# Two-layer encoder trunk: x's norms one group earlier, the second layer's rotary tables under the output projection, six weight tiles in flight between the layers

## The chip, the cores and the metric

The kernel runs on one core of a Trainium2 chip. The metric is the time of one execution on the device in microseconds (us). Its engines are named as the profile names them: PE (TensorE, matmuls), PEld (its weight loads), DVE (VectorE), ACT (ScalarE), POOL (GpSimd) and SP (SyncE, which here only issues transfers). Each engine takes its own instructions strictly in the order in which the program lists them, and waits where one needs a result that is not there yet.

## What is computed

Input x is 512 tokens of 1024 float32 values; there are 256 memory tokens. Each of two layers normalises x, multiplies it by one input projection, attends, gates the heads' outputs and adds an output projection to x:

```python
for i in range(DEPTH):                      # DEPTH = 2
    h = rmsnorm(x, norm_g[i])
    mem_h = rmsnorm(mem, mem_norm_g[i])
    if i % 2 == 0:
        proj = h @ w_in_a                   # 3 x 3 x 8 heads of 128, q_mem, gate
        o_mix = mixer_dilated(qkv, qn_a, kn_a, ang_a)
    else:
        proj = h @ w_in_b                   # 8 query heads, 2 kv heads, q_mem, gate
        o_mix = mixer_axial_gqa(q, k, v, qn_b, kn_b, ang_b)
    o_mem = memory_attention(q_mem, mem_h, w_mem_kv[i], ...)   # 4 heads
    y = concatenate([o_mix, o_mem]) * silu(gate)
    x = x + y @ w_out[i]
```

The rotary tables of the second layer are products of cosines and sines with the gains `qn_b` and `kn_b`.

## The kernel before

**Products.** A float32 product is made of three passes on PE: an operand is split into a rounded part and a rest, and `mm3` (L164 to L166) multiplies high by high, high by low and low by high. A weight tile (128x1024) is loaded by an SP transfer (`wl`, L238), rounded by ACT (`wh`, L287) and its rest is made by DVE (`wo`, L297). L164 and L166 need `wh`; L165 needs `wo`. Four pairs of `wh` and `wo` exist at a time.

**Seven products instead of eight.** Each projection of 512 columns is a Strassen-like scheme (`s_chunk`): seven products on quarters, in the order 12, 11, S1, S2, S4, S3, 22. Sums of weight quarters are made by accumulating transfers of POOL. Sums of the activation's quarters are made once per layer: `first_t` (quarters 12 and 11, tokens blocks 0 and 1), `diffs_t` (L531 makes S1, L532 makes S3, token blocks 2 and 3) and `rest_t` (L544 makes S2, L545 makes S4; then ACT rounds each at L539 and DVE makes its rest at L540). S1, S2, S3 and S4 are called `fS`, `f` and after rounding `hS` in the profile's rows. ACT copies a finished bank (`sn`, L364) and DVE adds into such a copy (`sn`, L381). The bank of product 11 is used again by S2, which therefore waits for L381.

**The order of the work.** Nothing reorders instructions after the program is written. A small driver does it while the program is built: after each group of PE matmuls it advances a slot counter, and generators that are due write their next piece into the engines' queues. `yield n` means "go on n slots later". What stands in one slot and what in the next thus sets each engine's order.

**The start.** Four groups of 12 matmuls make the memory keys, four the memory values (`mem_kv`, `proj_t`, operand `act`), while `prep` normalises the four token blocks of x: `norm_1` squares and sums on ACT (`sq`, L462) and gets the inverse root on POOL, `norm_2` scales on DVE (`x`, L469). PE then transposes a block (`xT`, L475, eight transposes into two PSUM buffers), ACT rounds it (L158) or copies it (L522, L527), and DVE makes the rest (L161). Between these PE also transposes the memory keys (`qT`, L571, one PSUM buffer each, read by ACT L619 and DVE L620). `xT` and `qT` share four PSUM buffers named `at`. `ahead` runs hooks inside the first four groups.

**Between the layers.** The output projection (`out_proj`) is a seven-product chunk with `y` and then two chunks on the third quarter of `y` (`out_rest`, results added at L739). Then come the second layer's memory keys and values, and the first chunk of its input projection. The second layer's tables (`setup_b`, one product at L1262 and four at L1265) are made on DVE in slots after the output projection.

**Weights in flight.** `KEEP` gives, by kind of chunk, how many weight tiles may be loaded and not yet used: `O1` is `out_rest`, `T2b` the second layer's memory keys and values.

Of the kernel before, what the change touches and what calls it, by code (L numbers as in the profile page):

```python
# [21 lines left out]
TCKW = {}  # L22
NBIG, NM4, NS2, SCRATCH = 7, 23, 13, 2048
RING, LEAD = 4, 2
BULK, ACTIVE, SET_AT, WARM, MEM_B, PREP_Y, ACC_AT, PREP_B, HALF, SET_B = 2, 2, 15, 1, 12, 1, 4, 1, {"a": 3, "b": 3, "o": 0}, 1
MEM_STEP = 1, 1
MEM_D = 4
PD = 2
# [7 lines left out]

SEQ = [1, 2, 0] + list(range(3, len(PLAN)))
T1_DMA = 17
KEEP = {"T2": 8, "T2b": 4, "O1": 4, "W1": 9, "W2": 10, "W2s": 9, "W1b": 7, "W2b": 9}


class Driver:
# [83 lines left out]
def trunk_kernel(ctx: ExitStack, tc: tile.TileContext, x, mem, wall, norm_g, mem_norm_g, gcol,  # L126
# [14 lines left out]
    def m4(dt=F32, name="m4"):  # L141
        return pool.tile([128, 1024], dt, tag="m4", name=name, bufs=NM4)
# [213 lines left out]
    def s_chunk(n, act, ev, tokens=True, pre=None, half=False, soon=False):  # L356


        units, per = n // 256, 1024 // n
        bank, snap = [None, None], {}  # L360

        def keep(name, u, b):
            t = snap[name, u] = s2(name="sn")
            A.copy(t, b)  # L364
            yield 1
            if name == "s3":
                diff(u)
                yield 1
                yield from ev("22", u, snap["s5", u])

        def diff(u):

            if (u, "22") not in snap:
                c = snap[u, "22"] = snap["s5", u]
                V.tensor_tensor(c, c, snap["s3", u], ALU.subtract)  # L375

        def add(q, name, u, b):
            t = snap[name, u]
            if name == "s3":
                diff(u)  # L380
            V.tensor_tensor(t, b, t, ALU.subtract if q == "12" else ALU.add)  # L381
            yield 1
            yield from ev(q, u, t)

        after = ((keep, "z"), (add, "11", "z"), (keep, "s5"), (keep, "s2"), (add, "12", "s2"), (keep, "s3"), (add, "21", "s3"))
        for i, (a, s, fresh) in enumerate(PRODUCTS):
            while a not in act:
                drv.tick()
            if fresh:
                bank[s] = [pj() for _ in range(units)]  # L390
            for x in range(units):
                wh, wo = [t.rearrange("p (k c) -> p k c", c=n) for t in W.take()]
                ah, al = act[a][:, 0], act[a][:, 1]
                for b in range(2):
                    if pre and i == x == 0 and b:
                        pre()
                    if half and b:
                        n_half[0] += 1
                        if n_half[0] % half == 0:
                            drv.half()  # L400
                    o = bank[s][b] if units == 2 else bank[s][0][:, b * 256:(b + 1) * 256]
                    bs = slice(b * 128, (b + 1) * 128)
                    for k in range(per):
                        kk = x * per + k
                        st, sp = fresh and kk == 0 and (units == 2 or b == 0), kk == 3
# [61 lines left out]
    def norm_2(xb, r, row, js=(0, 1)):  # L467
        for j in js:
            V.scalar_tensor_tensor(xb[j], xb[j], r, row[j], ALU.mult, ALU.mult)  # L469
# [65 lines left out]
    def rest_t(H, c, ds):  # L535

        def put(k, f):
            hi, lo = slot(H, k, c)
            A.copy(hi, f)  # L539
            drv.late(lambda: V.tensor_tensor(lo, f, hi.bitcast(F32), ALU.subtract))  # L540
# [12 lines left out]
        yield 1  # L553
# [24 lines left out]
    def halves(t):  # L578
        return [t[:, 0:512], t[:, 512:1024]]
# [261 lines left out]

        return gate, prep_y, YW, ys

    def out_proj(YW, ys, src, evac, tiles, half=False):

        acc, done = {}, set()

        def load():
            for i in range(2):
                for u, t in enumerate(tiles()):  # L850
                    nc.sync.dma_start(t, src[2 * i + u])
                    acc[2 * i + u] = halves(t)
                yield 2

        def ev(q, u, t):
            b, n = 2 * (int(q[0]) - 1) + u, int(q[1]) - 1
# [15 lines left out]
    rows = {}  # L872
# [17 lines left out]
        if c % 2:  # L890
            W.dma(2)
    H, H2 = {}, {}
    xb = [halves(t) for t in xt]
# [58 lines left out]
    def ahead(u, b):  # L952

        if (u, b) == (0, 1):
            for j in range(2):
                A.copy(rows["x"][j], gain[j])
            norm_3(mb[1], M, 128, 0)
            for c in range(2):
                norm_2(mb[c], nst[c], first, (1,))
        if (u, b) == (1, 0):  # L960
            for c in range(2):
                norm_3(mb[c], M, 128 * c, 1)
# [283 lines left out]
                yield EO[2]  # L1246
                yield from rest_t(H2, b - 2, EO[3:])

    drv.spawn(mem_norm(1), MEM_B)
    out_proj(YW, ys, xv, ev_o, lambda: [m4(name="acc") for _ in range(2)])  # L1250

    ropeB = pool.tile([128, 2048], F32, tag="tabs", name="tabs", bufs=1).rearrange("p (a c b e) -> p a c b e", a=2, c=2, b=4)
    tb_raw = s2(name="tbraw").rearrange("p (c b e) -> p c b e", c=2, b=4)
    nc.sync.dma_start(tb_raw, tab_b.rearrange("p (c b e) -> p c b e", c=2, b=4))
    grB = s2(name="grB")[:, 0:256].rearrange("p (a e) -> p a e", a=2)
    nc.sync.dma_start(grB[:, 0], qn_b.to_broadcast([128, 128]))
    nc.sync.dma_start(grB[:, 1], kn_b.to_broadcast([128, 128]))

    def setup_b():
        V.tensor_scalar(grB[:, 0], grB[:, 0], QS, None, ALU.mult)  # L1262
        for qk in range(2):
            for cs_ in range(2):
                V.tensor_tensor(ropeB[:, qk, cs_].rearrange("p b (h e) -> p b h e", h=2),  # L1265
                                tb_raw[:, cs_, :, None, :].to_broadcast([128, 4, 2, 64]),
                                grB[:, qk].rearrange("p (h e) -> p h e", h=2)[:, None].to_broadcast([128, 4, 2, 64]), ALU.mult)
# [45 lines left out]
    def rope_b(t, qk, i, d):  # L1313

        def v(x):
            return x.rearrange("p (b h e) -> p b h e", b=2, h=2)

        ta, sb = s2(name="ta"), s2(name="sb")
        V.tensor_tensor(v(ta), v(t), ropeB[:, qk, 0, 2 * i:2 * i + 2, None, :].to_broadcast([128, 2, 2, 128]), ALU.mult)
        V.tensor_tensor(v(sb), v(t), ropeB[:, qk, 1, 2 * i:2 * i + 2, None, :].to_broadcast([128, 2, 2, 128]), ALU.mult)  # L1320
# [235 lines left out]
```

## Time and profile before

| | us |
|---|---|
| three timed runs | 968.25, 972.17, 972.54 |
| their median | 972.17 |
| the profiled execution | 966.39 |
| span of its instructions | 964.6 |

The span runs from the first to the last instruction of the profiled execution; 1.8 us of it lie outside. A row of the timeline gives the start, the duration, the engine, the line, the operation, what is written and read, and in brackets the idle time just before it and what ended it. Rows merged as "x2" are two instructions back to back. A view by windows gives each engine's busy time in a stretch with the number of instructions, the granted clock of PE as a share of full speed, the share of the transfer engines in use and GB/s.

### The profile page before, as it was taken

Reading aid. Unit: us, or ns where it says so; the run is one execution under the profiler, and the core shown is the slowest. Engines: PE = TensorE matmul, PEld = TensorE weight load, DVE = VectorE, ACT = ScalarE, POOL = GpSimd, SP = SyncE. Lnnn points to the kernel's source line nnn. Section 1 sums busy time; section 2 is a strip of 40 time slices with the busy share of each in tenths; the row PEclk is TensorE's granted clock in tenths of the full one; section 3 lists DMA queues with packets and bytes.
Section 4 is the critical chain, followed back from the end, with each engine's and each line's share of the span. In section 5 each row is a group of like instructions: output and inputs, shape, how many; then the busy total and the mean of one; then the engine's idle time right before and its main releaser. Section 6 shows DMA issues by size and latency. Waiting matters only on the chain.

```text
span 964.6 us, 16613 instructions
## 1 busy us (share of the span) xinstructions
PE 947.5 (98%) x5682; PEld 833.3 (86%) x5682; DVE 790.6 (82%) x1411; ACT 683.0 (71%) x1701; POOL 339.7 (35%) x482
## 2 busy tenths in 40 slices
PE   8999999999999999999999999999899999999998
PEld 5879888888888888888899997888899999998876
DVE  4898676888888888888797999879888997779873
ACT  5874689686868686868675767556778887878760
POOL 1512523556454545464726011323233231011011
PEclk9999999999999999999999999999999999999999
DMA  9799946869686868685858989969976696877744
GB/s 361 234 285 341 288 112 177 288 123 265 147 259 151 258 155 261 154 262 132 269 147 216 276 194 281 310 198 308 284 174 148 175 239 163 222 202 173 191 144 131
DMA packets 89130, 209.81 MB, mean 218 GB/s; under 512 B 25299, under 2 KB 36051, under 8 KB 89045
## 3 DMA queue, kind: packets, MB, share of 16 engines
q1 hardware_dynamic: 69892, 145.76, 43.6%
q0 software_dynamic: 17856, 60.83, 33.7%
q10 hardware_dynamic: 1296, 2.16, 0.6%
q8 instruction: 45, 0.74, 0.3%
q14 instruction: 41, 0.33, 0.1%
HBM read 157.27 MB, written 12.65 MB: 176 GB/s over the span
## 4 chain that ended last, share of the span: by engine, by line
PE 86%; DVE 8%; ACT 3%; DMA 2%; issue 1%; SPq 0%; DVEq 0%; ACTq 0%
PE pj L166 22%; PE pj L164 22%; PE pj L165 22%; DVE wo L297 3%; PE qT L571 2%; PE sa L1089 1%; PE oo L1191 1%; PE pt L1170 1%; PE sa L1085 1%; PE ptb L1388 1%; DMA og<-odb 1%; PE xT L475 1%; PE ob L165 1%; PE row L592 1%; PE ob L166 1%
## 5 line engine op out<-in xcount | busy, mean ns | idle before, releaser
L297 DVE TENSOR_TENSOR wo<-wl,wh 128x1024 fp32r<-128x1024 f32 x255 | 314.2, 1238 | 5.8 <-ACT wh L287 5.7
L287 ACT CAST wh<-wl 128x1024 fp32r<-128x1024 f32 x255 | 269.2, 1059 | 55.9 <-PE pj L166 33.7
L164 PE MATMUL pj<-wh,hS 128*128 128x512 f32 (+1 forms) x448 | 164.3, 367 | 0.0
L165 PE MATMUL pj<-wo,hS 128*128 128x512 f32 (+1 forms) x448 | 158.8, 355 | 4.4 <-DVE wo L297 4.4
L166 PE MATMUL pj<-wh,hS 128*128 128x512 f32 (+1 forms) x448 | 158.7, 354 | 0.0
L164 PE MATMUL pj<-wh,h 128*128 128x512 f32 (+1 forms) x336 | 122.4, 364 | 0.0
L166 PE MATMUL pj<-wh,h 128*128 128x512 f32 (+1 forms) x336 | 118.5, 353 | 0.0
L165 PE MATMUL pj<-wo,h 128*128 128x512 f32 (+1 forms) x336 | 118.4, 352 | 0.1
L424 POOL TENSOR_TENSOR rstd<-mse,half 128x4 f32<-128x4 f32 (+2 forms) x98 | 102.2, 1043 | 8.2
L165 PEld LDWEIGHTS pj<-wo,hS 128*128 128x128 f32 x448 | 85.7, 191 | 15.3 <-DVE wo L297 5.3
L166 PEld LDWEIGHTS pj<-wh,hS 128*128 128x128 f32 x448 | 85.5, 191 | 12.2
L164 PEld LDWEIGHTS pj<-wh,hS 128*128 128x128 f32 x448 | 85.5, 191 | 10.4 <-ACT sn L364 0.4
L364 ACT COPY sn<-pj 128x512 f32<-128x512 f32 x132 | 73.9, 590 | 22.8 <-PE pj L166 19.2
L423 POOL TENSOR_SCALAR mse<-hss 128x4 f32<-128x4 f32 (+1 forms) x86 | 44.1, 513 | 124.0 <-ACT junk L559 120.2
L559 ACT ACTIVATE junk<-sn 128x128 f32<-128x128 f32 x264 | 79.0, 308 | 1.7 <-DVE sn L375 1.7
L1033 POOL TENSOR_TENSOR ta<-sn,tabs 128x128 f32<-128x128 f32 (+1 forms) x64 | 37.0, 579 | 120.0 <-DVE sn L564 91.6
L381 DVE TENSOR_TENSOR sn<-pj,sn 128x512 f32<-128x512 f32 x99 | 67.5, 684 | 5.4 <-PE pj L166 5.0
L166 PEld LDWEIGHTS pj<-wh,h 128*128 128x128 f32 x336 | 63.5, 189 | 8.9
L165 PEld LDWEIGHTS pj<-wo,h 128*128 128x128 f32 x336 | 63.7, 190 | 8.0 <-DVE wo L297 0.8
L164 PEld LDWEIGHTS pj<-wh,h 128*128 128x128 f32 x336 | 63.7, 190 | 7.2
L271 POOL DMA_DIRECT2D wl<-wl x33 | 29.1, 881 | 115.3 <-DVE wo L297 64.4
L164 PE MATMUL pj<-hS,wh 128*128 128x256 f32 x192 | 55.9, 291 | 0.0
(231 smaller groups left out, 2464.3 us busy)
## 6 DMA issues: line engine op xcount, KB each, us to landing
wl<-in_wall_dram SPq DMA_DIRECT2D x222, 512.0 KB, 7.0
wl<-wl POOLq DMA_DIRECT2D x66, 512.0 KB, 6.2
wl<-in_wall_dram POOLq DMA_DIRECT2D x42, 512.0 KB, 8.4
acc<-sn POOLq DMA_DIRECT2D x16, 256.0 KB, 5.2
od<-o SPq DMA_DIRECT2D x12, 256.0 KB, 5.8
og<-od SPq DMA_DIRECT2D x12, 256.0 KB, 6.8
odb<-o SPq DMA_DIRECT2D x12, 256.0 KB, 3.0
og<-odb SPq DMA_DIRECT2D x12, 256.0 KB, 4.5
```

The source lines that it names most:

```text
L164: T.matmul(o, lh, rh, start=start, stop=False, skip_group_check=True)
L165: T.matmul(o, lh, rl, start=False, stop=False, skip_group_check=True)
L166: T.matmul(o, ll, rh, start=False, stop=stop, skip_group_check=True)
L271: G.dma_start(self.tile[key], self.tile[c, "T2", x], accum_op=ALU.add)
L287: A.copy(wh, self.tile[self.items[i]])
L297: V.tensor_tensor(wo, self.tile[key], wh.bitcast(F32), ALU.subtract)
L364: A.copy(t, b)
L381: V.tensor_tensor(t, b, t, ALU.subtract if q == "12" else ALU.add)
L423: G.tensor_scalar(e, ss, EPS, None, ALU.add)
L424: G.tensor_tensor(r, e, half[:, 0:n], ALU.pow)
L559: A.activation(jk, p[:, j * 128:(j + 1) * 128], AF.Square, scale=QS, accum_out=ss[:, j:j + 1])
L1033: G.tensor_tensor(ta[:, 0:n], xn[:, 0:n, 0:32], ropeA[:, 0, b, s0:s0 + n], ALU.mult)
```

## The change

Four things are changed.

1. The first block's `norm_1` moves out of `prep` into `ahead`, after the first group. `prep` then has one step less, so each of its later pieces (scaling, transposes, rounding, differences) comes one group of matmuls sooner.
2. In `rest_t` the sum S4 (L545) moves behind the first `yield`: it is made in the slot in which it is rounded, in both layers.
3. `setup_b`, with its three table loads, is started inside `out_proj`, after the seven products, and its arithmetic begins three slots later (`SET_B` is 3 instead of 1). It runs under `out_rest` instead of under the second layer's memory keys.
4. `KEEP` of `O1` and `T2b` is 6 instead of 4.

```diff
-BULK, ... HALF, SET_B = ..., {"a": 3, "b": 3, "o": 0}, 1
+BULK, ... HALF, SET_B = ..., {"a": 3, "b": 3, "o": 0}, 3
...
-KEEP = {"T2": 8, "T2b": 4, "O1": 4, "W1": 9, ...}
+KEEP = {"T2": 8, "T2b": 6, "O1": 6, "W1": 9, ...}
...
         V.tensor_tensor(s2_, s1, s2_, ALU.subtract)
-        V.tensor_tensor(s4, s4, s2_, ALU.add)
         put("S2", s2_)
         yield ds[0]
+        V.tensor_tensor(s4, s4, s2_, ALU.add)
         put("S4", s4)
...
         s_chunk(512, YW, ev, half=half)
+        if side:
+            drv.spawn(side())
         out_rest(ys, acc, done, evac)
...
     def prep():
-        n = {}
-        for c in range(5):
+        for c in range(1, 5):
             if c < 4:
-                n[c] = norm_1(xb[c])
-            if c:
-                norm_2(xb[c - 1], n[c - 1], rows["x"])
+                nx[c] = norm_1(xb[c])
+            norm_2(xb[c - 1], nx[c - 1], rows["x"])
             if 1 < c < 4:
                 first_t(H, xb[c - 2], c - 2)
             yield 1
...
                 A.copy(rows["x"][j], gain[j])
+            nx[0] = norm_1(xb[0])
             norm_3(mb[1], M, 128, 0)
...
     def setup_b():
+        ropeB.append(pool.tile([128, 2048], F32, tag="tabs", ...))
+        tb_raw = s2(name="tbraw")...
+        nc.sync.dma_start(tb_raw, ...)
+        ...
+        yield SET_B
         V.tensor_scalar(grB[:, 0], grB[:, 0], QS, None, ALU.mult)
...
-    drv.spawn(setup_b(), SET_B)
+    drv.spawn(mem_norm(1), MEM_B)
+    out_proj(YW, ys, xv, ev_o, ..., side=setup_b)
```

What this does to the engines' queues is shown at three places. The first is DVE near the start, around the second half of the memory tokens' transposes (`act`); `x` is a token block being scaled. Before:

```order
L297 TENSOR_TENSOR wo<-wl,wh 128x1024 x2
L161 TENSOR_TENSOR act<-xT,act 128x4x128 x2
L469 SCALAR_TENSOR_TENSOR x<-x,rstd,row 128x512 x2
L297 TENSOR_TENSOR wo<-wl,wh 128x1024 x2
L469 SCALAR_TENSOR_TENSOR x<-x,rstd,row 128x512 x2
L161 TENSOR_TENSOR h_341<-xT,h_341 128x4x128
```

and in the changed kernel:

```order
L297 TENSOR_TENSOR wo<-wl,wh 128x1024 x2
L469 SCALAR_TENSOR_TENSOR x<-x,rstd,row 128x512 x2
L161 TENSOR_TENSOR act<-xT,act 128x4x128 x2
L469 SCALAR_TENSOR_TENSOR x<-x,rstd,row 128x512 x2
L161 TENSOR_TENSOR h_304<-xT,h_304 128x4x128
L161 TENSOR_TENSOR h_312<-xT,h_312 128x4x128
L297 TENSOR_TENSOR wo<-wl,wh 128x1024 x2
```

The first block of x is now scaled ahead of the memory tokens' rests, and the next weight pair stands behind two more pieces of x.

The second place is PE at the end of the memory values, around the second `qT`. Before:

```order
L166 MATMUL pj<-wh,act 128x512
L571 MATMUL qT<-ident,xn 128x128 x4
L164 MATMUL pj<-wh,h_341 128x512
L165 MATMUL pj<-wo,h_341 128x512
L166 MATMUL pj<-wh,h_341 128x512
```

and in the changed kernel:

```order
L166 MATMUL pj<-wh,act 128x512
L475 MATMUL xT<-ident,x 128x128 x8
L571 MATMUL qT<-ident,xn 128x128 x4
L164 MATMUL pj<-wh,h_304 128x512
L165 MATMUL pj<-wo,h_304 128x512
L166 MATMUL pj<-wh,h_304 128x512
```

The fourth token block's transposes, which stood 12 matmuls later, now come ahead of the second `qT`.

The third place is DVE where the second layer's first input chunk begins. `f_7907` and `f_7909` in turn hold S4, `hS` its rounded form, `wo` the weights of product S1 and of S2. Before:

```order
L544 TENSOR_TENSOR f_7909<-fS_8032,f_7909 128x4x128
L545 TENSOR_TENSOR f_7907<-f_7907,f_7909 128x4x128
L540 TENSOR_TENSOR hS_8069<-f_7909,hS_8069 128x4x128
L643 SCALAR_TENSOR_TENSOR vm<-pj,vm 128x512
L297 TENSOR_TENSOR wo<-wl,wh 128x1024 x2
L620 SCALAR_TENSOR_TENSOR kmT<-qT,gc,kmT 128x4x128
L540 TENSOR_TENSOR hS_8152<-f_7907,hS_8152 128x4x128 x2
L381 TENSOR_TENSOR sn<-pj,sn 128x512
```

and in the changed kernel:

```order
L544 TENSOR_TENSOR f_7911<-fS_8032,f_7911 128x4x128
L540 TENSOR_TENSOR hS_8068<-f_7911,hS_8068 128x4x128
L643 SCALAR_TENSOR_TENSOR vm<-pj,vm 128x512
L297 TENSOR_TENSOR wo<-wl,wh 128x1024 x2
L620 SCALAR_TENSOR_TENSOR kmT<-qT,gc,kmT 128x4x128
L547 TENSOR_TENSOR f_7909<-f_7909,f_7911 128x4x128
L540 TENSOR_TENSOR hS_8151<-f_7909,hS_8151 128x4x128
L547 TENSOR_TENSOR f_7909<-f_7909,f_7911 128x4x128
L540 TENSOR_TENSOR hS_8151<-f_7909,hS_8151 128x4x128
L381 TENSOR_TENSOR sn<-pj,sn 128x512
```

Both sums S4 (L545, now L547) have left the stretch ahead of the weight pair and stand between it and `sn`, each directly ahead of the rest that is made from its rounded form.

More of the change, by code (lines that the diff above doesn't have):

```diff
@@ L24 @@
 RING, LEAD = 4, 2
-BULK, ACTIVE, SET_AT, WARM, MEM_B, PREP_Y, ACC_AT, PREP_B, HALF, SET_B = 2, 2, 15, 1, 12, 1, 4, 1, {"a": 3, "b": 3, "o": 0}, 1
+BULK, ACTIVE, SET_AT, WARM, MEM_B, PREP_Y, ACC_AT, PREP_B, HALF, SET_B = 2, 2, 15, 1, 12, 1, 4, 1, {"a": 3, "b": 3, "o": 0}, 3
 MEM_STEP = 1, 1
@@ L38 @@
 T1_DMA = 17
-KEEP = {"T2": 8, "T2b": 4, "O1": 4, "W1": 9, "W2": 10, "W2s": 9, "W1b": 7, "W2b": 9}
+KEEP = {"T2": 8, "T2b": 6, "O1": 6, "W1": 9, "W2": 10, "W2s": 9, "W1b": 7, "W2b": 9}
 class Driver:
@@ L842, in gates, with out_proj @@
         return gate, prep_y, YW, ys
-    def out_proj(YW, ys, src, evac, tiles, half=False):
+    def out_proj(YW, ys, src, evac, tiles, half=False, side=None):
         acc, done = {}, set()
@@ L892, in trunk_kernel @@
     H, H2 = {}, {}
-    xb = [halves(t) for t in xt]
+    xb, nx = [halves(t) for t in xt], {}
     def prep():
-        n = {}
-        for c in range(5):
+        for c in range(1, 5):
             if c < 4:
-                n[c] = norm_1(xb[c])
-            if c:
-                norm_2(xb[c - 1], n[c - 1], rows["x"])
+                nx[c] = norm_1(xb[c])
+            norm_2(xb[c - 1], nx[c - 1], rows["x"])
             if 1 < c < 4:
@@ L1247, in ev_o @@
                 yield from rest_t(H2, b - 2, EO[3:])
[L1249 to L1259, printed above, removed]
-    def setup_b():
+    ropeB = []
+    def setup_b():
+        ropeB.append(pool.tile([128, 2048], F32, tag="tabs", name="tabs", bufs=1).rearrange("p (a c b e) -> p a c b e", a=2, c=2, b=4))
+        tb_raw = s2(name="tbraw").rearrange("p (c b e) -> p c b e", c=2, b=4)
+        nc.sync.dma_start(tb_raw, tab_b.rearrange("p (c b e) -> p c b e", c=2, b=4))
+        grB = s2(name="grB")[:, 0:256].rearrange("p (a e) -> p a e", a=2)
+        nc.sync.dma_start(grB[:, 0], qn_b.to_broadcast([128, 128]))
+        nc.sync.dma_start(grB[:, 1], kn_b.to_broadcast([128, 128]))
+        yield SET_B
         V.tensor_scalar(grB[:, 0], grB[:, 0], QS, None, ALU.mult)
@@ L1264, in setup_b @@
             for cs_ in range(2):
-                V.tensor_tensor(ropeB[:, qk, cs_].rearrange("p b (h e) -> p b h e", h=2),
+                V.tensor_tensor(ropeB[0][:, qk, cs_].rearrange("p b (h e) -> p b h e", h=2),
                                 tb_raw[:, cs_, :, None, :].to_broadcast([128, 4, 2, 64]),
@@ L1268, in setup_b @@
                 yield 1
-    drv.spawn(setup_b(), SET_B)
+    drv.spawn(mem_norm(1), MEM_B)
+    out_proj(YW, ys, xv, ev_o, lambda: [m4(name="acc") for _ in range(2)], side=setup_b)
     od_b = dram.tile([12, 128, S], F32, name="odb", bufs=1)
@@ L1318, in rope_b @@
         ta, sb = s2(name="ta"), s2(name="sb")
-        V.tensor_tensor(v(ta), v(t), ropeB[:, qk, 0, 2 * i:2 * i + 2, None, :].to_broadcast([128, 2, 2, 128]), ALU.mult)
-        V.tensor_tensor(v(sb), v(t), ropeB[:, qk, 1, 2 * i:2 * i + 2, None, :].to_broadcast([128, 2, 2, 128]), ALU.mult)
+        V.tensor_tensor(v(ta), v(t), ropeB[0][:, qk, 0, 2 * i:2 * i + 2, None, :].to_broadcast([128, 2, 2, 128]), ALU.mult)
+        V.tensor_tensor(v(sb), v(t), ropeB[0][:, qk, 1, 2 * i:2 * i + 2, None, :].to_broadcast([128, 2, 2, 128]), ALU.mult)
         yield d[1]
```

## The prediction

> **What bounds the kernel now.** I read the page first, then PE's waits, then a table of stretches, then the timeline of the stretches in which PE waits.
>
> ```profile
> PE 947.5 (98%) x5682; PEld 833.3 (86%) x5682; DVE 790.6 (82%) x1411; ACT 683.0 (71%) x1701; POOL 339.7 (35%) x482
> PE pj L165 <- DVE wo L297: 5.0, 4, 2.9
> PE row L592 <- DMA row<-in_mem_norm_g_dram: 2.4, 1, 2.4
> core 0: us, PE busy (x) PEld busy (x) DVE busy (x) ACT busy (x) POOL busy (x), PEclk, DMA share, GB/s
> 18.00:64.00 46.00, 44.06 (x208) 34.67 (x209) 42.63 (x56) 36.17 (x76) 17.01 (x22) 1.00 0.88 271
> 575.00:626.00 51.00, 49.63 (x236) 39.77 (x235) 46.06 (x74) 31.32 (x51) 11.34 (x15) 1.00 0.98 293
> 626.00:670.00 44.00, 44.00 (x221) 36.95 (x222) 35.28 (x48) 25.47 (x57) 14.65 (x22) 1.00 0.77 247
> 670.00:690.00 20.00, 17.15 (x131) 16.95 (x130) 18.04 (x25) 16.41 (x31) 4.48 (x6) 0.91 1.02 318
> ```
>
> PE is busy 98% of the span, so a microsecond counts only where PE waits, and PE waits mostly for `wo`, which DVE makes: four waits, 5.0 us. They lie where DVE has no room: it is busy 42.6 of 46 us in 18 to 64, and 18.0 of 20 us in 670 to 690. Between 626 and 670 PE loses nothing and DVE has 8.7 us to spare. So the change is worth what it does to DVE's order in the first and the last of these stretches.
>
> **Part 1, the start.** Moving block 0's norm costs ACT two squares, which fit into its idle time ahead of the first row below. The other pieces of `prep` go one group up. These rows price them:
>
> ```profile
> 17.43 0.59 ACT L158 CAST act<-xT 128x512 fp32r<-128x512 f32 x1 [4.31 <-PE xT L475]
> 19.96 2.35 DVE L297 TENSOR_TENSOR wo<-wl,wh 128x1024 fp32r<-128x1024 f32 x2
> 22.44 1.29 DVE L161 TENSOR_TENSOR act<-xT,act 128x512 fp32r<-128x512 f32 x2
> 23.65 1.41 DVE L469 SCALAR_TENSOR_TENSOR x<-x,rstd,row 128x512 f32<-128x512 f32 x2
> 23.19 0.50 PE L166 MATMUL pj<-wh,act 128*128 128x512 f32 x1
> 23.53 0.39 PE L164 MATMUL pj<-wh,act 128*128 128x512 f32 x1
> 23.76 0.40 PE L165 MATMUL pj<-wo,act 128*128 128x512 f32 x1
> ```
>
> DVE rows that follow each other overlap by about 0.08, so a weight pair takes 2.27, a pair of x 1.33, a pair of rests 1.21, a single 128x512 piece 0.6. A matmul takes 0.23, the first after a wait 0.34. Today the `act` pair begins at 22.44 and PE's L166, which reads it, at 23.19. With x's pair ahead (22.23 to 23.56) the `act` pair begins at 23.56 and L166 at 24.30: **1.1 us** of new wait.
>
> How long DVE then takes up to the weights of product S1 follows from these rows of DVE and ACT, whose instructions are the same in the new order:
>
> ```profile
> 33.11 2.35 DVE L297 TENSOR_TENSOR wo<-wl,wh 128x1024 fp32r<-128x1024 f32 x2
> 35.38 1.22 DVE L256 TENSOR_TENSOR wl<-wl 128x1024 f32<-128x1024 f32 x1
> 32.03 1.18 ACT L522 COPY f<-xT 128x512 f32<-128x512 f32 x2 [0.27 <-DVE h L161]
> 33.11 0.28 ACT L559 ACTIVATE junk<-pj 128x128 f32<-128x128 f32 x1
> 35.34 1.10 ACT L158 CAST h<-xT 128x512 fp32r<-128x512 f32 x2
> 39.63 2.00 ACT L287 CAST wh<-wl 128x1024 fp32r<-128x1024 f32 x2
> ```
>
> From 24.30 PE needs 2.4 us for its ten remaining matmuls (0.34 + 9 x 0.23), then transposes block 0; ACT's rounding starts at 27.3, DVE's rests at 27.9. DVE goes on: rests 29.15, weight pair 31.4, block 2 32.75. Then it waits for ACT's rounding of block 1, which stands behind two copies (from 28.7, 1.08), four `junk` and two squares (33.11 to 35.34, 2.23) and a weight pair (1.9): ACT reaches it at 33.9, DVE at 34.5. Rests 35.7, `xn` 36.3, weight pair 38.55, L256 39.7, block 3 41.0, `xn` 41.6, L256 42.7, weight pair 45.0. There stand L531 and L532, at 45.0 and 45.6.
>
> ```profile
> 42.45 0.60 PE L571 MATMUL qT<-ident,xn 128*128 128x128 f32 x4
> 45.99 1.03 PE L475 MATMUL xT<-ident,x 128*128 128x128 f32 x8
> 45.62 0.68 DVE L531 TENSOR_TENSOR fS<-xT,f 128x512 f32<-128x512 f32 x1
> 46.98 0.69 DVE L161 TENSOR_TENSOR hS<-fS,hS 128x512 fp32r<-128x512 f32 x1
> 48.06 0.69 DVE L643 SCALAR_TENSOR_TENSOR vm<-pj,vm 128x512 fp32r<-128x512 f32 x1 [0.39 <-ACT vm L642]
> 48.67 2.35 DVE L297 TENSOR_TENSOR wo<-wl,wh 128x1024 fp32r<-128x1024 f32 x2
> 47.92 0.59 ACT L527 COPY f<-xT 128x512 f32<-128x512 f32 x1
> 56.83 0.50 PE L165 MATMUL pj<-wo,hS 128*128 128x512 f32 x1 [0.88 <-DVE wo L297]
> 60.51 0.50 PE L165 MATMUL pj<-wo,hS 128*128 128x512 f32 x1 [0.67 <-DVE wo L297]
> ```
>
> Here a second wait is new. Transposes share four PSUM buffers. In the new order block 2 holds two, the first `qT` one (its readers L619 and L620 come later), and block 3 now takes the fourth and the one that ACT's L527 has freed. The second `qT` must wait for the last reader of block 2's other buffer, L532, which ends at 46.3. PE would be there at 42.45 + 1.1 + 0.8 (block 3's transposes, now ahead of it) = 44.35: **2.0 us** of new wait.
>
> From L531 on, the rows give 2.44 to the first `vm` (45.62 to 48.06), so it is at 47.45. Behind it now stand `kmT`, L544 and an L540 whose rounding on ACT comes after a weight pair and a copy (ACT is free 0.14 before `vm`: 47.3 + 1.9 + 0.5 + 0.6, so DVE at 50.35), then `vm` after two more ACT pieces (51.4) and only then product 11's weight pair, at 52.0. Its 2.27, `kmT` 0.66, the 1.36 from L531 to L161 (ACT rounds between), L161's 0.6, another such 1.36 from L545 to its L540, with L544 inside, and two L540 at 0.6 put S1's first weight at 59.5 and PE's L165 at 60.75 (1.27 later, as 677.53 to 678.80 in part 2). Today that is 56.83, and the second weight's matmul is at 60.51. In the new order its weight is in time, 12 matmuls later (0.34 + 11 x 0.23): 63.6. Today's waits in 18 to 64 (46 less 44.06, 1.9 us) go, longer ones come: **net +3.1 us**. After it PE is bound by itself until 575, so nothing wins this back.
>
> If the buffers fell otherwise, the 2.0 would shrink, but DVE's walk would still end at 60.75; only a shorter walk helps. Its two waits for ACT (27.9 and 34.5) are the uncertain ones; 0.5 us either way.
>
> **Part 2, the tables and S4.**
>
> ```profile
> 658.46 1.29 DVE L161 TENSOR_TENSOR h<-xT,h 128x512 fp32r<-128x512 f32 x2 [2.14 <-ACT h L158]
> 659.66 0.68 DVE L1265 TENSOR_TENSOR tabs<-tbraw,grB 128x512 f32<-128x512 f32 x1
> 677.53 2.35 DVE L297 TENSOR_TENSOR wo<-wl,wh 128x1024 fp32r<-128x1024 f32 x2
> 679.80 0.74 DVE L620 SCALAR_TENSOR_TENSOR kmT<-qT,gc,kmT 128x512 fp32r<-128x512 f32 x1
> 680.46 1.28 DVE L540 TENSOR_TENSOR hS<-f,hS 128x512 fp32r<-128x512 f32 x2
> 681.66 0.68 DVE L381 TENSOR_TENSOR sn<-pj,sn 128x512 f32<-128x512 f32 x1
> 678.80 0.39 PE L165 MATMUL pj<-wo,hS 128*128 128x256 f32 x1 [2.85 <-DVE wo L297]
> 683.14 0.28 PE L164 MATMUL pj<-wh,hS 128*128 128x256 f32 x1
> 676.00:680.00 4.00, 1.20 (x7) 1.20 (x8) 3.62 (x5) 4.00 (x7) 0.00 (x0) 0.90 1.04 269
> 680.00:684.00 4.00, 4.00 (x26) 4.00 (x26) 4.00 (x7) 1.47 (x4) 0.00 (x0) 0.67 1.04 286
> ```
>
> Four table products leave DVE's queue (2.6 us with the scaling of the gain). Three stand ahead of a 2.14 us idle wait for ACT, which swallows them; only the one at 659.66 counts, 0.6. The first L545, 0.6 like it, now comes later and gives 0.6 more; the second lies in a wait for ACT's `vm`. So the weights of S1 come 1.2 earlier and the wait of 2.85 falls to 1.65. The tables' new place is the stretch 626 to 670, with 8.7 us of room on DVE: nothing.
>
> But S2 uses the bank of product 11 again and waits for DVE's `sn`. Behind the weight pair (now 676.3 to 678.6) come `kmT` (679.25), L545, a round trip to ACT before its L540 (1.36, as L531 to L161), L540, and the same once more: 679.25 + 1.36 + 0.6 + 1.36 + 0.6 = 683.2, and `sn` ends at 683.85. S2 starts at 683.9 instead of 683.14: **+0.8**. PE then waits there for 3.5 us, since S1's 24 matmuls (half as wide, about 0.12 each, 2.9) end at 680.4.
>
> **The clock.** Today's wait of 2.85 us cost more than itself: the clock fell to 0.90 and 0.67 in the two windows above, 0.10 x 4 + 0.33 x 4 = 1.7 us lost, hidden in part under the same `sn`. A wait of 3.5 us should do it again, right after S2 has started, where nothing hides it: **+1.6**. The Trainium skill, "TensorE: Matmul & The Clock Gate", Part 1, has the clock halved only after a whole idle window of a free-running 3.4 us: the wait of 2.85 us, shorter than that, contradicts it here. By that rule 3.5 us would hardly ever hold a whole window and the sum would lack this term; that is rival A.
>
> **Six weights in flight.** The only transfer in PE's list of waits is the first row's at the start, so earlier loads gain nothing. Two more 0.52 MB loads in a stretch at 293 GB/s are up to 3.6 us of transfers ahead of the gates' reads; those reads end none of PE's waits today, so I take 0 and keep +1 for the range.
>
> **Sum.** 3.1 + 0.8 + 1.6 = **+5.5 us**: the profiled execution would be 971.9 instead of 966.39. That execution lies 5.8 below the median of the runs shown; the terms are waits inside the program and carry over, so 972.17 + 5.5 = **977.7 us**. About 0.5% (4.9 us) is what a measurement of this kernel can tell from no change.
>
> **Rivals.**
> - A, the clock stays full: 3.1 + 0.8 = +3.9, 976.1. For it: the waits at 56.83 and 60.51 (0.9 and 0.7) left it full. Against: 2.85 did not. Chance 0.22.
> - B, the clock falls at the start too, where 2.0 us of wait lie between 1.2 us of transposes: 1.7 more, +7.2, 979.4. Chance 0.10.
> - C, faster: `qT` finds a free buffer and DVE's new order keeps ahead of PE, as the move would have it. Then the waits in 18 to 64 (1.9), 1.2 at S1 and the part of the clock's loss that `sn` didn't hide (0.7) go: -3.8, 968.4. It decides if DVE has S1's weight before 55.5. Against it: DVE had 3.4 us of idle time in that whole stretch, and the new order puts two more round trips to ACT ahead of product 11's weights. Chance 0.08, with its bounds half of it past 0.5%.
> - D, no change: the moved work sits under PE as it did, 972.2. Chance 0.10.
>
> The forecast keeps 0.50, with 976.5 to 979. Slower by over 0.5%: 0.44 of it, 0.10 from B, 0.04 from A: 0.58. Faster 0.04, the rest 0.38. The range, with the scatter of the runs (4.3 us) and the bounds above: 972.0 to 981.5.
>
> **What would show it.** L166 at about 24.3 waiting for `act`; a wait of 2 us ahead of the second `qT`, released by L532; L165 of S1 near 60.75; the wait for `wo` at S1 of the second layer down to 1.65, followed by one of 3.5 at S2, released by L381; PEclk under 1 just after. If PE reaches product S2 of the first chunk no later than today, the first term is wrong, and with it the sign.

## The result and the profile after

The changed kernel takes 975.97 us in the median of 9 runs (973.82 to 980.87), the kernel before 969.84 in 9 runs beside it (966.12 to 974.64). The ratio is 1.0064, with a 95% interval of 1.0038 to 1.0091: slower by about 6 us. The profiled execution of the changed kernel took 977.56, its span is 975.8.

The first row is the busy list of the page of the changed kernel; the others are its table of stretches (length, busy time and count for PE, PEld, DVE, ACT and POOL, then the granted clock, the DMA share and GB/s), cut where the program is at the same places as in the prediction's table.

```profile
PE 952.4 (98%) x5682; PEld 837.1 (86%) x5682; DVE 790.4 (81%) x1411; ACT 682.6 (70%) x1701; POOL 340.3 (35%) x482
18.00:64.00 46.00, 41.50 (x194) 33.30 (x195) 40.09 (x52) 32.38 (x68) 15.15 (x19) 0.96 0.84 265
577.00:634.00 57.00, 53.44 (x245) 42.31 (x244) 49.70 (x79) 34.13 (x55) 12.49 (x18) 0.97 0.98 285
634.00:678.00 44.00, 44.00 (x222) 36.94 (x221) 35.21 (x49) 26.11 (x59) 13.54 (x21) 1.00 0.75 228
678.00:700.00 22.00, 16.78 (x116) 16.40 (x115) 16.39 (x22) 14.94 (x29) 4.50 (x6) 0.84 1.00 289
```

The start loses what was forecast. From 678 to 700 PE stands idle 5.2 us of 22. Between them a stretch has grown that the prediction did not touch, the output projection. The waits themselves, from the timeline of PE in the changed kernel (start, duration, what it does, and in brackets the idle time ahead and what ended it):

```profile
24.52 0.50 PE L166 MATMUL pj<-wh,act 128*128 128x512 f32 x1 [1.10 <-DVE act L161]
46.73 0.63 PE L571 MATMUL qT<-ident,xn 128*128 128x128 f32 x4 [2.00 <-DVE fS L532]
61.08 0.50 PE L165 MATMUL pj<-wo,hS 128*128 128x512 f32 x1 [0.88 <-DVE wo L297]
586.62 0.50 PE L165 MATMUL pj<-wo,y 128*128 128x512 f32 x1 [0.79 <-DVE wo L297]
626.31 0.50 PE L164 MATMUL pj<-wh,y 128*128 128x512 f32 x1 [0.47 <-ACT y L784]
628.13 0.55 PE L166 MATMUL pj<-wh,y 128*128 128x512 f32 x1 [1.09 <-DVE y L786]
686.99 0.58 PE L165 MATMUL pj<-wo,hS 128*128 128x256 f32 x1 [3.06 <-DVE wo L297]
693.43 0.55 PE L164 MATMUL pj<-wh,hS 128*128 128x256 f32 x1 [2.16 <-ACT hS L539]
```

The first three are the forecast's, to 0.3 us. The next three are not in it. The wait at S1 (686.99) was to fall to 1.65 and has not.

Two profiled executions differ by more than the change: before's took 966.39 where its runs have a median near 970. So the comparison below goes by stretches over all profiles, experiments included. Each number is the distance between the starts of two matmuls that every kernel has (or, for the last, to the end of the span). **Start**: the L164 at 22.46 in before, ahead of the one that waits, to the first transpose at L700 (134.40). **Out**: the first matmul with `y` (573.55) to the second layer's first transpose of the memory (625.25). **12 to S1**: the first matmul of the second layer's product 12 (669.83) to S1's first L165 (678.80). **S1 to S2**: on to S2's first L164 (683.14). **After S2**: on to the first `om` (735.42). **Last**: the last matmul into `ob` (929.09) to the end (964.6).

| kernel | start | out | 12 to S1 | S1 to S2 | after S2 | last |
|---|---|---|---|---|---|---|
| before | 111.94 | 51.70 | 8.97 | 4.35 | 52.27 | 35.52 |
| part 1 alone | 115.00 | 53.40 | 10.97 | 5.07 | 52.74 | 35.68 |
| part 1, scaling behind | 113.87 | 52.57 | 8.98 | 4.29 | 52.27 | 35.61 |
| six weights alone | 111.99 | 53.70 | 8.96 | 4.36 | 52.26 | 34.18 |
| tables alone | 111.96 | 54.29 | 8.82 | 4.05 | 52.56 | 35.46 |
| S4 alone | 112.48 | 52.46 | 8.24 | 6.45 | 53.63 | 35.54 |
| tables and six | 111.96 | 52.85 | 9.98 | 4.35 | 52.27 | 34.18 |
| six, S1 filled | 111.97 | 53.04 | 8.98 | 3.69 | 52.34 | 34.22 |
| changed, S4 back | 114.95 | 52.68 | 9.50 | 5.07 | 52.58 | 34.18 |
| changed | 115.20 | 56.26 | 9.18 | 6.44 | 53.79 | 34.19 |
| changed, again | 115.02 | 55.61 | 9.00 | 6.44 | 52.34 | 34.24 |
| changed, four weights | 115.01 | 55.83 | 8.81 | 6.45 | 53.82 | 35.57 |
| changed, filled | 115.18 | 55.01 | 8.75 | 6.44 | 52.34 | 34.19 |
| changed, filled again | 115.08 | 55.60 | 9.60 | 6.45 | 52.34 | 34.21 |

Three columns split clearly: the start goes with part 1 (+3.1; S4's move alone adds 0.5), "S1 to S2" with S4's move (6.44 or 6.45 with it, 3.69 to 5.07 without), "last" with six weights (-1.3). "Out" scatters by more than 2 us, and before's 51.70 is the lowest of all.

### The profile page after: what moved, and what is told of

It is laid out like the page before. It is cut to its first block, busy times and chain, and to the rows that moved or that the text cites. A ratio compares the mean times of both kernels' runs of the same rounds, so it can differ in the third digit from the quotient of the medians.

```text
span 975.8 us, 16620 instructions
## 1 busy us (share of the span) xinstructions
PE 952.4 (98%) x5682; PEld 837.1 (86%) x5682; DVE 790.4 (81%) x1411; ACT 682.6 (70%) x1701; POOL 340.3 (35%) x482
## 3 DMA queue, kind: packets, MB, share of 16 engines
q10 hardware_dynamic: 1296, 2.16, 0.6%
## 5 line engine op out<-in xcount | busy, mean ns | idle before, releaser
L164 PE MATMUL pj<-wh,hS 128*128 128x512 f32 (+1 forms) x448 | 165.0, 368 | 2.2 <-ACT hS L539 2.2
L165 PE MATMUL pj<-wo,hS 128*128 128x512 f32 (+1 forms) x448 | 159.3, 356 | 3.9 <-DVE wo L297 3.9
L166 PE MATMUL pj<-wh,hS 128*128 128x512 f32 (+1 forms) x448 | 159.2, 355 | 0.0
L164 PE MATMUL pj<-wh,h 128*128 128x512 f32 (+1 forms) x336 | 122.9, 366 | 0.0
L166 PE MATMUL pj<-wh,h 128*128 128x512 f32 (+1 forms) x336 | 119.2, 355 | 0.0
L165 PE MATMUL pj<-wo,h 128*128 128x512 f32 (+1 forms) x336 | 118.8, 354 | 0.0
L424 POOL TENSOR_TENSOR rstd<-mse,half 128x4 f32<-128x4 f32 (+2 forms) x98 | 104.2, 1063 | 8.2
L165 PEld LDWEIGHTS pj<-wo,hS 128*128 128x128 f32 x448 | 86.3, 193 | 14.5 <-DVE wo L297 4.5
L164 PEld LDWEIGHTS pj<-wh,hS 128*128 128x128 f32 x448 | 86.1, 192 | 12.5 <-ACT wh L287 2.3
L166 PEld LDWEIGHTS pj<-wh,hS 128*128 128x128 f32 x448 | 86.1, 192 | 12.3
L166 PEld LDWEIGHTS pj<-wh,h 128*128 128x128 f32 x336 | 63.9, 190 | 9.1
L165 PEld LDWEIGHTS pj<-wo,h 128*128 128x128 f32 x336 | 64.1, 191 | 7.5
L164 PEld LDWEIGHTS pj<-wh,h 128*128 128x128 f32 x336 | 64.1, 191 | 7.4
L164 PE MATMUL pj<-hS,wh 128*128 128x256 f32 x192 | 55.9, 291 | 0.0
```

The costliest lines, as they stand in the source:

```text
L164: T.matmul(o, lh, rh, start=start, stop=False, skip_group_check=True)
L165: T.matmul(o, lh, rl, start=False, stop=False, skip_group_check=True)
L166: T.matmul(o, ll, rh, start=False, stop=stop, skip_group_check=True)
L424: G.tensor_tensor(r, e, half[:, 0:n], ALU.pow)
```

## Experiments

### Each part alone

Part 1 alone: the hunks of `prep` and `ahead`. Six weights alone:

```diff
-"T2b": 4, "O1": 4
+"T2b": 6, "O1": 6
```

Tables alone: `setup_b` under `out_proj`, `SET_B` 3. S4 alone:

```diff
-        V.tensor_tensor(s4, s4, s2_, ALU.add)
         put("S2", s2_)
         yield ds[0]
+        V.tensor_tensor(s4, s4, s2_, ALU.add)
```

> The kernel before with part 1 alone (norm of block 0 ahead of the first product, the rest of prep one group up); tables, S4 and the number of weights in flight as before. Theory 1 (part 1 costs what its own new waits cost, and nothing later wins it back): the profile has L166 after a wait of about 1.3 us at 24.5, a wait of about 2.1 ahead of the second qT, S1's first L165 at 61 instead of 56.83, and PE is 3.5 us later than before at every place from there to 575; ratio about 1.0035, +3 to +4 us. Theory 2 (slack behind the start, in the steady stretch, takes it back): the same waits, but ratio 1.000 to 1.001. Theory 3 (the clock's fall at 48 is a part of the changed kernel's loss that belongs to part 1): PEclk 0.5 for 3.4 us near 48 here as well; without it the sum would be near 3.1 all the same, since product 12 at full speed would only wait for wo instead.

> The kernel before with six instead of four weights in flight between the layers, nothing else. Theory 1 (the extra loads ahead of the row, the two m and the od write make these land later, and the gates' last og read with them): the od write takes about 4.5 us instead of 2.4, DVE waits about 3 us for og (0.57 before), PE loses 1 to 2 us near 620, and if the clock falls on it 1.6 more; ratio 1.001 to 1.004. Theory 2 (the prediction: these transfers end none of PE's waits): ratio 1.000, PE's waits between 575 and 670 as before.

> The kernel before with the tables of the second layer multiplied beneath the output product, nothing else. Theory 1 (DVE sets S1's weight in the second layer): the wait of 2.85 us at L165 falls by 0.6 to about 2.2; ratio 0.999, -0.6 us, up to -1.5 if the clock then stays full. Theory 2 (ACT's rounding of that weight waits for a transfer, wl<-wl, so that DVE's earlier arrival changes nothing): the wait stays at 2.5 to 3.1 and DVE waits for ACT's hS there; ratio 1.000. Theory 3 (the tables' and gains' loads, now ahead of the og reads or of x's writes, delay these): a new wait of 0.5 to 2 us near 620; ratio 1.001 to 1.003.

> The kernel before with S4's addition moved behind S2's rounding, nothing else; this also moves it in the first layer's start. Theory 1 (prediction): S1's weight in the second layer comes up to 0.6 earlier, S2 starts 0.8 later behind sn and waits there for about 3 us, and the clock falls once more after it: +0.8 to +2.4, ratio 1.001 to 1.0025. Theory 2 (the wait only changes its place): ratio 1.000. At the start DVE makes the same pieces in another order; S1's L165 within 0.7 of 56.83.

| alone | median | ratio to before (969.85) | 95% interval |
|---|---|---|---|
| part 1 | 972.76 | 1.0030 | 1.0012 to 1.0048 |
| six weights | 967.59 | 0.9984 | 0.9969 to 0.9999 |
| tables | 969.40 | 0.9995 | 0.9980 to 1.0009 |
| S4 | 972.73 | 1.0035 | 1.0015 to 1.0054 |

Part 1 costs 2.9 us in the runs and 3.1 in its stretch: nothing wins it back. The interval does not tell the tables' gain from nothing, and the stretches say why: S1 comes only 0.15 sooner (8.97 to 8.82), and the 0.30 won from S1 to S2 (4.35 to 4.05) comes back behind S2 (52.27 to 52.56), because the half clock begins 0.9 us later after S1. This is theory 2 of the third expectation: with the tables alone ACT waits for a transfer, as in this row of its timeline.

```profile
676.10 1.05 ACT L287 CAST wh<-wl 128x1024 fp32r<-128x1024 f32 x1 [0.74 <-DMA wl<-wl]
```

S4's move costs about as much as part 1, 2.9 us between the medians and 3.4 by the ratio, above the 0.8 to 2.4 expected. In the table it is 0.5 at the start, 1.4 up to S2 and 1.4 behind S2. Its rows, from the timeline of PE in the kernel with S4 alone:

```profile
678.85 0.39 PE L165 MATMUL pj<-wo,hS 128*128 128x256 f32 x1 [2.13 <-DVE wo L297]
685.30 0.55 PE L164 MATMUL pj<-wh,hS 128*128 128x256 f32 x1 [3.43 <-ACT hS L539]
```

The wait at S1 falls by 0.7, as forecast (0.6), and one of 3.43 stands at S2. The second row names ACT's `hS`; but in the same kernel DVE's `sn` ends only just before it:

```profile
683.86 0.69 DVE L540 TENSOR_TENSOR hS<-f,hS 128x512 fp32r<-128x512 f32 x1 [0.69 <-ACT hS L539]
684.47 0.68 DVE L381 TENSOR_TENSOR sn<-pj,sn 128x512 f32<-128x512 f32 x1
```

`sn` ends at 685.15, S2 starts at 685.30: the bank that `sn` reads is the last thing missing. ACT's rounding ends just then, too; but in the kernel with six weights and S1 filled (below), where ACT's `hS` is done 1.7 us earlier, S2 follows the end of `sn` by the same 0.15. The 0.69 ahead of L540 is the round trip to ACT that the move has put there; it stands there twice, once for each sum.

Six weights alone come out ahead, against both theories, if barely (the interval ends at 0.9999). The gain is at the end. From the timelines of DVE, first before, then with six weights:

```profile
936.05 1.36 DVE L781 TENSOR_TENSOR sn<-sn,og 128x512 f32<-128x512 f32 x2 [4.06 <-DMA og<-odb]
```

```profile
936.48 1.50 DVE L781 TENSOR_TENSOR sn<-sn,og 128x512 f32<-128x512 f32 x2 [2.49 <-DMA og<-odb]
```

In before SP issues one more weight load between the last write of the heads' output and its reading back; with six in flight that load has gone out earlier, the reading lands sooner, and PE's wait in the last product is gone (none is left there with six). This is that wait, in before:

```profile
940.41 0.50 PE L166 MATMUL pj<-wh,y 128*128 128x512 f32 x1 [1.04 <-DVE y L786]
```

Between the layers the same setting does the reverse. SP waits for the write `od` before it reads it back; this is that wait in the output projection (total, times, longest), first before, then with six weights:

```profile
SPq L763 <- DMA od<-o: 1.6, 1, 1.6
```

```profile
SPq L763 <- DMA od<-o: 4.3, 1, 4.3
```

Six loads instead of four go out ahead of that write. In all eight profiles with six weights the reading is issued 3.7 to 5.3 us after the write, in the six with four weights 2.2 to 2.8. PE pays for it one step later, at `y`, as theory 1 expected, in the kernel with six weights alone:

```profile
619.20 1.38 DVE L781 TENSOR_TENSOR sn<-sn,og 128x512 f32<-128x512 f32 x2 [2.76 <-DMA og<-od]
622.43 0.50 PE L166 MATMUL pj<-wh,y 128*128 128x512 f32 x1 [1.10 <-DVE y L786]
```

### What the changed kernel is without S4's move, and the gains together

S4's sum put back ahead of S2 in the changed kernel; and, apart from it, tables and six weights alone.

> The changed kernel with S4's addition back ahead of S2's rounding; part 1, tables and six weights as in it. Theory 1 (S4's move costs 3 to 3.5 us as measured alone, by a later sn, a wait at S2 and one more half-clock window): +1 to +2.5 us against before, ratio 1.001 to 1.0025; no wait over 0.5 us at S2 of the second layer. Theory 2 (S4's cost is swallowed in the changed kernel by the late weight at S1): ratio still 1.005 to 1.0065.

> The kernel before with the tables beneath the output product and six weights in flight together, without part 1 and without S4's move. Theory 1 (the parts add: -0.5 and -1.5 us measured alone): ratio 0.9975 to 0.9985, a mean of 1.4 half-clock windows in an execution. Theory 2 (six in flight gained nothing; the 0.16% was scatter): ratio 0.999 to 1.000. Theory 3 (the loads of the tables and two more weights together end the gates' last read late, and that is what the changed kernel lost between 575 and 632): a wait of 1 to 2 us near 620 in the profile and a ratio above 1.000.

Without S4's move the changed kernel takes 972.62, 1.0027 (1.0008 to 1.0046), about what theory 1 said, and no wait is left at S2: by the ratios more than half of the loss goes with one addition that has changed places with a rounding, though the two intervals overlap. Tables and six weights together take 968.91, 0.9989 (0.9968 to 1.0009), not to be told from before; of the three theories on them it excludes none, and the wait at `y` near 620 is 0.7 us, under the 1 to 2 of theory 3.

### Is the start set by DVE's walk or by PE's waits?

Part 1, but block 0's scaling stands behind the `act` pair, as before:

```diff
-            norm_2(xb[c - 1], nx[c - 1], rows["x"])
+            if c > 1:
+                norm_2(xb[c - 1], nx[c - 1], rows["x"])
...
                 norm_3(mb[c], M, 128 * c, 1)
+            norm_2(xb[0], nx[0], rows["x"])
```

> The kernel before with part 1, but with block 0's two scalings behind the act pair again, so that L166 does not wait; all other pieces of prep stay one group up. Theory 1 (prediction: DVE's walk, not PE's waits on the way, sets S1's weight): no wait at L166, the wait at the second qT grows from 2.1 to about 3.2, S1's L165 still at 60 to 61, ratio 1.003 like part 1 alone. Theory 2 (the two waits add): S1's L165 about 1.1 earlier, 59.7 less the scatter of the start, ratio 1.002.

PE's waits in this kernel and, below, with part 1 alone:

```profile
44.42 0.63 PE L571 MATMUL qT<-ident,xn 128*128 128x128 f32 x4 [1.99 <-DVE fS L532]
58.73 0.50 PE L165 MATMUL pj<-wo,hS 128*128 128x512 f32 x1 [0.92 <-DVE wo L297]
```

```profile
23.27 0.50 PE L166 MATMUL pj<-wh,act 128*128 128x512 f32 x1 [1.09 <-DVE act L161]
45.47 0.93 PE L571 MATMUL qT<-ident,xn 128*128 128x128 f32 x4 [1.98 <-DVE fS L532]
59.78 0.50 PE L165 MATMUL pj<-wo,hS 128*128 128x512 f32 x1 [0.94 <-DVE wo L297]
```

The wait at L166 is gone, the one at `qT` has not grown, and S1 comes 1.05 earlier, as theory 2 has it. DVE's walk is as long as before, but it begins earlier. These are DVE's rests of block 0, first in this kernel, then with part 1 alone:

```profile
25.88 1.29 DVE L161 TENSOR_TENSOR h<-xT,h 128x512 fp32r<-128x512 f32 x2 [0.48 <-ACT h L158]
```

```profile
26.92 1.29 DVE L161 TENSOR_TENSOR h<-xT,h 128x512 fp32r<-128x512 f32 x2 [1.79 <-ACT h L158]
```

DVE waits there for ACT's rounding of block 0, which PE transposes after L166. From there on each of its pieces up to S1's weight comes 1.04 to 1.07 earlier; all its longer waits are for ACT, and ACT's are for DVE. So what delays PE at L166 delays the walk, which theory 1 had left out. Whether the wait at `qT` delays S1 as well is not tested: it stands in both kernels. The median is 972.43, 1.0024 (1.0002 to 1.0047).

### What the clock costs

Every run lists its mean granted clock, and the profiles show that it is cut to one half for 3.41 us at a time, or twice that (a fall in the program's last microseconds runs past its end). With 1.71 us lost in each, the mean clock gives roughly their number: 1.5 in an execution of before, 2.1 with part 1 alone, 2.4 with S4 alone, 1.4 with either of the others, 3.3 in the changed kernel. Useless matmuls in front of S1 and S2 fill the waits:

```diff
+                if fill and i in fill and x == 0:
+                    o, r = (bank[s][0] if fresh else at("busy")), act["S1"][:, 0]
+                    for _ in range(fill[i]):
+                        T.matmul(o[:, 0:256], r[:, 0, 0:128], r[:, 0], start=True, stop=True)
...
-    s_chunk(256, H2, ev_qmb)
+    s_chunk(256, H2, ev_qmb, fill={2: 16, 3: 16})
```

> The changed kernel with 16 matmuls of no use, 128x256, put in front of S1's first and 16 in front of S2's first in the second layer, where PE otherwise stands idle; nothing of the result changes. Theory 1 (idle stretches of PE of over about 2 us drop the clock, and the dropped clock costs part of the loss): the waits there fall under 1.7 us each, the mean number of half-clock windows falls from 3.3 to about 1.5 to 2, and the median falls by 1 to 2.5 us, ratio 1.004 to 1.0055. Theory 2 (the halved clock lies under other waits and costs nothing): fewer windows, but ratio unchanged at 1.006. Theory 3 (the clock falls by other causes than idle time): windows still 3.

> The changed kernel once more, for a second profile and to stand beside the next run. Theory 1 (the 4.6 us that its first profile lost between the output product's start and the second memory norm, 577 to 633, are scatter of the transfers): this profile loses 0.5 to 3 us there and its span is 2 to 4 us shorter. Theory 2 (they belong to the change): 4 to 5 us there again. Ratio 1.005 to 1.007, 3.3 half-clock windows in the mean.

> The changed kernel with the 32 matmuls of no use again, on the same chip as the changed kernel itself. Theory 1 (the clock's fall behind S2 costs the 1.4 us that two profiles show and a third with the useless matmuls does not): 1 to 2 us below the run beside it, ratio 1.0035 to 1.0055, 1.5 to 2 half-clock windows. Theory 2 (what the clock loses lies under DVE's work anyway): the same time as the run beside it, within 0.7 us.

The first time the filled kernel took 975.41, 1.0070 (1.0047 to 1.0093), with 1.65 half-clock stretches in the mean; beside the changed kernel on one chip it took 974.24 against 976.22, 1.0048 (1.0031 to 1.0065) against 1.0073 (1.0054 to 1.0092), with 1.3 against 3.3. At S1 and S2 the clock falls because PE idles: with the waits filled neither profile has a fall there. The second profile of the changed kernel loses 3.9 us in "out" against before's, as the first lost 4.6, and its span is only 0.7 shorter: that loss is no scatter of one execution. The 2 us between the second pair are what theory 1 said, the first run shows none of it, and the intervals overlap: the runs alone leave the price open.

The profiles are clearer. The four microseconds behind S2's start, from the tables of stretches of the changed kernel, of its second profile, and of the filled kernel:

```profile
693.00:697.00 4.00, 3.57 (x18) 3.60 (x19) 4.00 (x6) 4.00 (x13) 0.00 (x0) 0.57 0.95 339
```

```profile
692.75:696.75 4.00, 4.00 (x33) 4.00 (x34) 4.00 (x6) 4.00 (x13) 0.25 (x1) 1.00 1.01 334
```

```profile
691.50:695.50 4.00, 4.00 (x34) 4.00 (x35) 4.00 (x6) 4.00 (x14) 0.27 (x1) 1.00 0.71 277
```

18 matmuls at clock 0.57 against 33 and 34 at 1.00. In the table of stretches "after S2" is 53.6 to 53.8 in the three profiles in which the clock fell there, 52.3 in the three others with S4's move: 1.3 to 1.5 us. In the changed kernel's second profile it fell for 6.8 us from S1 on instead, and was back when S2 started; that fall cost nothing, since "S1 to S2" is 6.44 with it and without.

### Six or four weights in the changed kernel, and six with S1 filled

The second is the kernel before with six weights and `fill={2: 20}`, matmuls in front of S1 alone.

> The changed kernel with four weights in flight again. Theory 1 (six in flight saves 1.3 us at the last product and costs nothing between the layers): a wait of about 1.2 us ahead of a matmul of the last product with y, 1 to 1.5 us slower than the changed kernel beside it, ratio 1.0065 to 1.008. Theory 2 (the two more loads cost the changed kernel some 3 us between 577 and 633): 1 to 2 us faster than it, ratio 1.0035 to 1.005.

> The kernel before with six weights in flight and 20 matmuls of no use in front of S1 in the second layer; no part 1, no tables, no S4. Theory 1 (six in flight gains 1.3 us at the last product, the full clock behind S1 up to 0.8): ratio 0.997 to 0.9985, under 1 half-clock window in the mean. Theory 2 (the clock's fall at S1 lies wholly under sn): 0.9985 like six in flight alone.

With four weights the changed kernel takes 974.81, 1.0060 (1.0042 to 1.0077), beside 976.22 with six: neither theory is told from the other by the times. The profile gives theory 1 its 1.3 us at the last product, and "out" is 55.83, as large as with six: the 3 us there are not the six weights'. Six weights on the kernel before with S1 filled: 969.92, 1.0001 (0.9984 to 1.0018), above what both theories said, though its clock fell less (0.95 stretches) and "S1 to S2" is 0.7 shorter. So no version here beats before beyond doubt; six weights alone come nearest.

## Why the prediction was right, step by step

The time forecast was 977.7 us, 5.5 above the median of the three runs shown. Measured: 975.97, 6.1 above before. The three runs it started from lay 2.3 above the median of nine, which more than makes up the 1.7 between forecast and result. Sign and size were right; the sum was not right term by term, and that it came out so near is in part luck, as the terms at the end of this section show.

- **L166 at 24.30, 1.1 us of new wait.** Right: 24.52 with 1.10 of wait; this execution's start was 0.22 late.
- **Second `qT` waits 2.0 for L532.** Right: 2.00, released by L532.
- **S1's L165 at 60.75, net +3.1.** Right: 61.08 less the 0.22, and 111.94 to 115.0 or 115.2 over the whole start. The walk was right as well: the two waits of DVE for ACT that were put at 27.9 and 34.5 end at 28.18 and 34.77, as these rows of DVE in the changed kernel show.

```profile
28.18 1.29 DVE L161 TENSOR_TENSOR h<-xT,h 128x512 fp32r<-128x512 f32 x2 [1.80 <-ACT h L158]
34.77 1.29 DVE L161 TENSOR_TENSOR h<-xT,h 128x512 fp32r<-128x512 f32 x2 [1.70 <-ACT h L158]
```

- **"DVE's walk would still end at 60.75; only a shorter walk helps."** Not tested as it stands: it speaks of the wait at `qT`, which every kernel with part 1 has. A walk that begins earlier helps, too: taking away the wait at L166 brought S1 1.05 earlier. The prediction's own working allows that, since its walk is counted from L166 at 24.30.
- **The clock at the start (rival B, 1.7 more).** It fell, at 48.17 for 3.41 us, and cost nothing: the start is 115.08 in the one profile of the changed order without that fall and 115.0 to 115.2 with it. Without it PE waits instead, for product 11's weight and behind `sn`, as these rows of the timeline of PE in the filled kernel's second profile show:

```profile
52.12 0.50 PE L165 MATMUL pj<-wo,h 128*128 128x512 f32 x1 [0.55 <-DVE wo L297]
58.24 0.49 PE L164 MATMUL pj<-wh,hS 128*128 128x512 f32 x1 [0.59 <-ACT sn L364]
```

- **Tables 0.6, S4's addition 0.6 more, "the wait of 2.85 falls to 1.65".** Alone, S4's addition took 0.72 off the wait at S1, the tables only 0.15. With the tables moved, DVE came earlier and waited for ACT, and ACT for a transfer. These are rows of ACT and DVE in the changed kernel:

```profile
682.44 1.05 ACT L287 CAST wh<-wl 128x1024 fp32r<-128x1024 f32 x1 [1.83 <-DMA wl<-wl]
```

```profile
684.04 0.69 DVE L540 TENSOR_TENSOR hS<-f,hS 128x512 fp32r<-128x512 f32 x1 [2.26 <-ACT hS L539]
685.72 2.35 DVE L297 TENSOR_TENSOR wo<-wl,wh 128x1024 fp32r<-128x1024 f32 x2
```

  The same wait of ACT, 1.4 to 2.3 us, stands in the profiles of part 1 alone, of tables and six weights, and of the changed kernel with S4 back. The transfer makes the sum for S2's weight, and ACT rounds that ahead of what DVE needs next. Its issue by POOL and its use by ACT (the second of the two) in before, and its issue in the changed kernel:

```profile
662.96 0.93 POOL L261 DMA_DIRECT2D wl<-wl  x1
672.94 1.99 ACT L287 CAST wh<-wl 128x1024 fp32r<-128x1024 f32 x2
```

```profile
671.61 0.92 POOL L261 DMA_DIRECT2D wl<-wl  x1
```

  In before it lands 8.2 us after its issue, some 2.8 before ACT takes it up; in the changed kernel it takes 10.7. All eight profiles with the tables moved issue it 6.2 us ahead of product 12 and have it 4.1 to 5.4 us after product 12 has begun, with ACT waiting for it. Of the six others five issue it 6.3 to 6.9 ahead and have it 1.1 to 3.6 after, with no wait; part 1 alone issues it 5.9 ahead and has it 6.4 after. So the late transfer goes with the tables' move. One or two weight loads of SP then go out ahead of it that in before go out after it; whether these slow it, and why POOL issues it later, no run shows. The step that failed is to have taken the weight's transfer as landed because in before it ended none of these waits.
- **S2 0.8 later.** Mis-sized by that same step: product 12 to S2 is 13.32 in before and 15.62 in the changed kernel, +2.3. For S4 alone the working gives 0.8 + 0.6 (no tables), 1.4, and 13.32 became 14.69. PE's own wait at S2 is 2.16 and not 3.5, since S1 comes later, and `sn` again ends 0.15 before S2 starts.
- **The clock after S2, +1.6.** Right where it happens (1.3 to 1.5), but it is not in every execution. The Trainium skill, "TensorE: Matmul & The Clock Gate", Part 1, asks for a whole idle window of 3.4 us; here the longest idle rows near the four falls are 2.00, 1.09, 3.06 and 2.16 us, all shorter, so that rule, which would have made rival A, does not hold here. The length of each fall, 3.41 us or twice that, agrees with its window.
- **Six weights, 0.** Wrong at both ends: -1.3 at the last product in every profile with them, and a reading of the heads' outputs that lands late between the layers. The reason given, "The only transfer in PE's list of waits is the first row's at the start", was the mistake: PE's list names the engine that came last (DVE's `y`), and the transfer stands one step behind it, in DVE's list.
- **Nothing between 575 and 632.** Wrong: "out" is 55.0 to 56.3 in the five profiles that have part 1, tables and S4's move together, and 51.7 to 54.3 in the nine others. Part of it are waits for `og` through `y`, part a fall of the clock in three of them, part waits for `wo` in its first 12 us (0.8 to 1.8 in three of them, 2.3 with the tables alone). It goes with neither the number of weights (55.83 with four) nor with part 1, tables and six weights alone (52.68). In the one profile with S4 back it is gone, although the instructions of that stretch and their order are then the same. The moment at which it begins does not tell them apart: 576.28 with S4 back, 575.53 to 577.25 in the five. No run shows why the transfers land later in it. It stays open.

So, against the typical execution, about 3.1 at the start, 1.9 to 2.7 at S2 over the five profiles of the changed kernel and its variants, 1.4 for the clock in some executions, some 3 us in "out" and -1.3 at the end. The forecast missed the last two, which are of opposite sign, and undersized the second. The start was right by its mechanism; that the whole came out right is luck as far as these terms make up for one another.

## What to carry to other kernels

When an engine is made earlier, look up what its next input waits for, and whether that is a transfer: here the gain of 1.2 us ended at one that in the kernel before landed 2.8 us ahead of its use, and that was late in every kernel with the tables moved. A list of waits names only the last releaser, so before a transfer is called free, read the list of the engine that PE waits for, too. And an instruction that is moved behind a rounding brings a round trip to another engine into the queue: each of the two trips (0.69 us of idle time) cost `sn` about as much as the addition itself (0.6).

## What the runs showed of the hardware

In the changed kernel's profile the granted clock falls after idle stretches of PE well under 3 us (2.00 us ahead of the fall at 48.17, 2.16 ahead of the one at 693.29), even after two short ones close together (0.47 and 1.09 us, with two matmuls between them, ahead of the fall at 628.44). A fall cost 1.3 to 1.5 us behind S2, where PE sets the pace, 0.7 at S1 of the kernel with six weights (4.36 against 3.69 when filled), and nothing at S1 of the changed kernel, where PE waits for `sn` anyway. So the mean clock of a run says how often PE idled rather than how much time was lost.
